# A condition-vector product moved from GpSimd columns to VectorE rows in a one-layer RWKV-7 block

## Chip, cores and metric

One core of one Trainium2 chip runs the whole kernel. The metric is device time in microseconds (us), the median of several executions; lower is better.

## The reference

One layer at width D = 2048, 512 tokens, all in float32: an RWKV-7 time mixer followed by a gated feed-forward layer with a causal convolution, each between two RMS norms. Both are modulated by a vector c:

```python
mod = jax.nn.silu(c) @ ada_w + ada_b          # ada_w: 2048 x 12288
sh_m, sc_m, g_m, sh_f, sc_f, g_f = jnp.split(mod + ada_table, 6)
h = rms(x, norm_mix_pre) * (1 + sc_m) + sh_m
y = rwkv7_mix(h)        # r, k, v = products 2048 x 2048; a scan over tokens with a 64 x 64 state per head; output product w_o
x = x + g_m * rms(y, norm_mix_post)
h = rms(x, norm_ffn_pre) * (1 + sc_f) + sh_f
x = x + g_f * rms(conv_ffn(h), norm_ffn_post)
```

The change is about `mod`: one vector times a matrix. Parts 0 and 1 (sh_m, sc_m) are needed at the start; parts 2 to 5 (g_m, sh_f, sc_f, g_f), 16 blocks of 128 channels each, are needed later and are computed beside other work.

## The kernel before, in words

Channels lie on the 128 partitions, tokens along the columns; KT = D/128 = 16. Each float32 product is made of three matmuls of halves: a weight tile is split into a high part (ScalarE, line 231) and a low part (line 233), and `mm3` (lines 276 to 278) multiplies high by high, high by low and low by high. Low parts are made by VectorE, but `wst["pool"] = 2` hands every second one to GpSimd during the state steps. Weights arrive in chunks of 512 KB through the SyncE queue (line 218).

After each `mm3` the function `tick()` advances a list of generators (`sides`) by one `yield`. Side work is placed in this way: so many ticks apart, in the order in which the code reaches it. The tile framework then orders the instructions of each engine; each engine and each DMA queue executes its own list in order, and an instruction that waits holds up those behind it. `behind()` puts an operation behind the last low part issued on VectorE.

The stages around the change: the v products (to about 300 us), the k products with the first half of the scan's preparation (`stage1`), the r products with the state steps (about 640 to 1150 us), the output product `wo`, then the feed-forward layer. In the r stage the loop over 16 blocks makes 16 r units and two gate units per block and copies the r product at line 1076. Beside it run: `inverse` (GpSimd, lines 774 and 776, small triangular inverses), `solve`, `transfer` (Gram matrices and masked copies on VectorE, lines 888 and 905) and `chain`. `chain` goes through 16 pairs of heads with eight chunks each; per chunk it multiplies the state (lines 927 and 935), scales it on ScalarE or VectorE in turn (lines 933 and 931), and yields twice. At the end of each pair `norm` begins with a square on ScalarE (line 948).

Parts 2 to 5 of `mod` come in two ways:

- `ada_jobs` (lines 460 to 508), on GpSimd. `on_pool(2048)` is 5: five groups of 512 channels, that is part 2 and a quarter of part 3. Partitions are the inputs of c. For each of 16 input blocks a 128 x 512 tile (256 KB, line 470) is loaded, multiplied by the partition's value of silu(c) (line 491; the first one at line 489) and added to a sum (line 492). The sum over partitions is four matmuls with a vector of ones (line 476) and an addition of the bias on VectorE (line 478). There are two load buffers, and four ticks between steps. It is started by `begin()` when the state steps start and must have ended at the `drain` in line 1116.
- `row_jobs` (lines 519 to 538), on VectorE. Partitions are 128 output channels and the columns are the inputs, from the transposed matrix `ada3`. One SCALAR_TENSOR_TENSOR (line 534) multiplies a row block by `crow`, the vector silu(c) on all partitions (loaded by `c_row`, line 513), and sums along the columns; line 535 adds the bias, or the earlier half. The 44 blocks that GpSimd doesn't have are made so: part 4 in the v stage (16 rows of 2048 columns), 12 rows of part 3 in the `wo` stage, part 5 at the feed-forward's output product (16 rows in two halves of 1024 columns, `in_halves`).

Of the kernel before, what the change touches and what calls it, by code (L numbers as in the profile page):

```python
# [10 lines left out]
F32 = mybir.dt.float32  # L11
F32R = mybir.dt.float32r
AF = mybir.ActivationFunctionType
ALU = mybir.AluOpType

T = 512
P = 128
# [14 lines left out]
VI = {n: i for i, n in enumerate(VEC_D)}  # L32


def on_pool(d):

    return d // min(512, d) * 2 * 5 // 8


def row_blocks(d):  # L40

    n = min(512, d) // P
    return [(vi, b) for vi in range(2, 6) for b in range(d // P) if ((vi - 2) * (d // P) + b) // n >= on_pool(d)]


class Cfg:
# [119 lines left out]
def body(ctx, tc, g, ap):  # L166
    nc = tc.nc
    KT, FT, GT, D = g.KT, g.FT, g.GT, g.D
    V, S, G, PE = nc.vector, nc.scalar, nc.gpsimd, nc.tensor
# [7 lines left out]
    def bank(i, shape=(P, T)):  # L177
        return pp.tile(list(shape), F32, tag=f"b{i}", name=f"bk{i}")
# [9 lines left out]
    ones = cp.tile([P, P], F32, name="ones")  # L188
# [9 lines left out]
    bt = cp.tile([P, 6, KT], F32, name="bt")  # L198
# [5 lines left out]
    cs = cp.tile([P, KT], F32, name="cs")  # L204
# [3 lines left out]
    mods = {q: cp.tile([P, KT], F32, name=f"mod{q}") for q in (2, 3, 4, 5)}  # L208
# [60 lines left out]
    def behind(on=True):  # L269

        return tc.issue_after(wst["last"].ins) if on else nullcontext()
# [178 lines left out]
    wst["pool"] = 0  # L450


    QC = min(512, D)
    QB = QC // P
    ROWS = row_blocks(D)

    def all_of(*vis):
        return [(vi, q) for vi in vis for q in range(D // QC)]

    def ada_jobs(pool, parts, bk, pace, bufs, eng=V, sums=1, get=None, last=False, to="ja"):  # L460

        todo = [(vi, q, k) for vi, q in parts for k in range(KT)]
        got = {}
        done = []

        def load(i):
            if i < len(todo):
                vi, q, k = todo[i]
                got[i] = get(i % bufs) if get else pool.tile([P, QC], F32, tag="js", name="js", bufs=bufs)
                nc.sync.dma_start(got[i], ap["ada2"][(vi - 2) * (D // QC) + q, :, k])  # L470

        def finish():
            vi, q, a = done.pop()
            ps = bank(bk)
            for b in range(QB):
                PE.matmul(ps[:, b:b + 1], a[:, b * P:(b + 1) * P], ones[:, 0:1], start=True, stop=True)
                yield
            V.tensor_tensor(mods[vi][:, q * QB:(q + 1) * QB], ps[:, 0:QB], bt[:, vi, q * QB:(q + 1) * QB], ALU.add)

        for i in range(bufs):  # L480
            load(i)
        yield
        for n, (vi, q, k) in enumerate(todo):
            if k == 0:
                a = pool.tile([P, QC], F32, tag=to, name="ja", bufs=sums)
            w, c = got.pop(n), cs[:, k:k + 1]
            with behind(last):
                if k == 0:
                    eng.tensor_scalar(a, w, c, None, ALU.mult)
                elif eng is G:  # L490
                    G.tensor_tensor(w, w, c.to_broadcast([P, QC]), ALU.mult)  # L491
                    G.tensor_tensor(a, a, w, ALU.add)  # L492
                else:
                    eng.scalar_tensor_tensor(a, w, c, a, ALU.mult, ALU.add)
            if eng is not G:
                load(n + bufs)
            if k >= KT // 2 and done:
                yield from finish()
            for _ in range(pace[n % len(pace)]):
                yield  # L500
            if eng is G:
                load(n + bufs)
            if k == KT - 1:
                done.append((vi, q, a))
        for _ in range(6):
            yield
        yield from finish()

    d_c = dram("d_c", (KT, P))

    part = cp.tile([P, KT], F32, name="part")
# [1 line left out]
    def c_row(t, cols=slice(0, D)):  # L513

        n = cols.stop - cols.start
        nc.sync.dma_start(t, d_c.rearrange("k p -> (k p)")[cols].unsqueeze(0).to_broadcast([P, n]))
        return t

    def row_jobs(todo, crow, get, bufs, pace, cols=slice(0, D)):

        got = {}

        def load(i):
            if i < len(todo):
                got[i] = get(i % bufs)
                nc.sync.dma_start(got[i], ap["ada3"][ROWS.index(todo[i])][:, cols])

        for i in range(bufs):
            load(i)
        yield  # L530
        for n, (vi, b) in enumerate(todo):
            w, to = got.pop(n), part[:, b:b + 1]
            with behind():
                V.scalar_tensor_tensor(w, w, 1.0, crow, ALU.mult, ALU.mult, accum_out=to)  # L534
            V.tensor_tensor(mods[vi][:, b:b + 1], to, mods[vi][:, b:b + 1] if cols.start else bt[:, vi, b:b + 1], ALU.add)
            load(n + bufs)
            for _ in range(pace):
                yield


# [42 lines left out]
    for b in range(nv0, KT - 2):  # L583
        ps = kinner("v", b, xv, bank(b % 2))
# [453 lines left out]
    s2_a, s2_b = transfer(), chain()  # L1038
    opened, jobs = [], []

    def begin():
        while fixed in sides or inv[0] in sides:
            yield
        ld_a[0], ld_b[0] = load_a(0), load_b(0)
        for i, hv in enumerate(HV):
            nc.sync.dma_start(LH[i][hv, :, HD - i * HD:P - i * HD], d_bnd[0][hv, :, 2 - 2 * i])
        while s1_last in sides:
            yield
        invert_ready(KT)
        ss_stack.close()  # L1050
        pool_of[0] = ss_stack.enter_context(tc.tile_pool(name="scn2", bufs=1))
        opened.append(True)
        wst["pool"] = 2
        ld_k[0] = load_k(0)
        yield from solve(0)
        load_v(0, 0)
        load_v(0, 1)
        jobs.append(ada_jobs(pool_of[0], [(g // (D // QC) + 2, g % (D // QC)) for g in range(on_pool(D))], 2, (4,), 2, G, 2))
        sides.extend((s2_a, s2_b, jobs[0]))

    sides.append(begin())
# [64 lines left out]
    def spare(tag, name, w=T):  # L1126
        return ap_.tile([P, w], F32, tag=tag, name=name)
# [77 lines left out]
    for b in range(KT - NL):  # L1205
        if b >= KT - NL - 4:
            fetch_x(*divmod(b - (KT - NL - 4), 2))
        ps = po[b] if b < n0 else kinner("wo", b, yx, bank((2, 6)[b % 2]))
        block_out(b, ps, acc1, yo[b], sqs[b % 2])
        if b == 1:  # L1210
            jobs = row_jobs([r for r in ROWS if r[0] < 4], c_row(spare("b2", "crow", D)),
                            lambda i: tp.tile([P, D], F32, tag=f"t3{'hl'[i]}", name="js"), 2, 8)
            sides.append(jobs)
    halves = [between(0), between(1)]
# [356 lines left out]
def layout(x):  # L1571
    D, F = x["x"].shape[-1], x["ffn_w_out"].shape[1]
    g = Cfg(D, F, x["rwkv_w1"].shape[2], x["rwkv_a1"].shape[2], x["rwkv_g1"].shape[2])
    KT, FT = g.KT, g.FT
    w = {s: x[n][0] for s, n in WMAP}
    w["r"], w["k"], w["v"] = x["rwkv_w_rkv"][0]
    tiles = np.zeros((g.nchunks * CH, P, P), np.float32)
    for i, key in enumerate(g.units):
        if key is None:
            continue  # L1580
        n, r, c = key
        t = w[n][r * P:(r + 1) * P, c * P:(c + 1) * P]
        tiles[i, :t.shape[0], :t.shape[1]] = t
    a = {"w": np.ascontiguousarray(tiles.reshape(g.nchunks, CH, P, P).transpose(0, 2, 1, 3).reshape(g.nchunks, P, CH * P))}
    ada = x["ada_w"].reshape(KT, P, 6, KT, P)
    a["ada1"] = np.ascontiguousarray(ada[:, :, 0:2].transpose(3, 1, 0, 2, 4).reshape(KT, P, KT, 2 * P))
    q = min(512, D)
    a["ada2"] = np.ascontiguousarray(
        x["ada_w"].reshape(KT, P, 6, D // q, q)[:, :, 2:].transpose(2, 3, 1, 0, 4).reshape(-1, P, KT, q)[:on_pool(D)])
    a["ada3"] = np.ascontiguousarray(np.stack([x["ada_w"][:, vi * D + b * P:vi * D + (b + 1) * P].T for vi, b in row_blocks(D)]))  # L1590
    cols = list(x["ada_b"].reshape(6, D)) + list(x["ada_table"][0].reshape(6, D))
    cols += [x[n][0] for n in ("norm_mix_pre", "norm_mix_post", "norm_ffn_pre", "norm_ffn_post")]
    cols += list(x["rwkv_mu"][0])
    cols += [x[n][0].reshape(D) for n in ("rwkv_w0", "rwkv_a0", "rwkv_k_k", "rwkv_k_a", "rwkv_r_k", "rwkv_ln_w", "rwkv_ln_b")]
    cols += [x["c"][0]]
    a["vec"] = np.ascontiguousarray(np.stack(cols).reshape(len(VEC_D), KT, P).transpose(2, 0, 1))
    f = np.concatenate([x["ffn_conv_w"][0], x["ffn_conv_b"]], 0)
    a["fvec"] = np.ascontiguousarray(f.reshape(4, 2 * FT, P).transpose(2, 0, 1))
    a["xT"] = np.ascontiguousarray(x["x"][0].T.reshape(KT, P, T))
    a["cst"] = CONST  # L1600
    return g, a
# [13 lines left out]
```

## Time and profile before

| what | value |
|---|---|
| median of 3 runs | 2754.91 us (2747.02 to 2760.35) |
| the profiled execution | 2750.25 us |
| its span in the trace | 2748.4 us |
| mean granted clock of the matrix unit | 0.979 |
| matrix unit (PE) busy | 2585.2 us (94%) |
| VectorE (DVE) busy | 2033.9 us (74%) |
| ScalarE (ACT) busy | 1329.8 us (48%) |
| GpSimd (POOL) busy | 810.1 us (29%) |

The span runs from the first to the last instruction; the profiled execution's own time is 1.85 us longer. PE is the matrix unit, PEld its weight load, DVE VectorE, ACT ScalarE, POOL GpSimd, SP SyncE; a q behind a name (SPq) is that engine's instruction queue, which issues DMAs. Matmuls are pipelined and their ends are modelled, so their busy time overstates how full the matrix unit is. In names, an arrow reads "output <- inputs": `js` is a loaded tile of the modulation matrix, `ja` a sum on GpSimd, `crow` the vector on all partitions, `wl` a low part, `wr` a loaded weight chunk, `bk` a bank of the matrix unit's results.

### The profile page before, as it was taken

How to read it: one execution, taken by the hardware profiler on the slowest of the kernel's cores; microseconds unless marked ns; L12 is line 12 of the kernel's file. 1: busy time of each engine (PE TensorE's matmuls, PEld its weight loads, DVE VectorE, ACT ScalarE, POOL GpSimd, SP SyncE). 2: the span in 40 equal slices, each digit the busy share in tenths (PEclk: the TensorE clock that was granted, in tenths of full speed). 3: DMA queues.
4: the chain of work that ended last, by engine and by line, in shares of the span. 5: the costliest groups of instructions: out<-in, count | busy, mean ns of one | idle time of the engine just before them, and what ended most of it. 6: DMA issues, size and time to landing. Idle time of an engine off the chain costs nothing.

```text
span 2748.4 us, 47108 instructions
## 1 busy us (share of the span) xinstructions
PE 2585.2 (94%) x17670; PEld 2263.7 (82%) x17670; DVE 2033.9 (74%) x3110; ACT 1329.8 (48%) x2313; POOL 810.1 (29%) x877
## 2 busy tenths in 40 slices
PE   5899999988999998999889999999999999999997
PEld 3568877776777776789779999999999988788896
DVE  5978688887666666657888888888887876544477
ACT  4442355553444445445665555555555553243464
POOL 3643114658787444500431211212111100000000
PEclk8999999999999999999999999999999999999998
DMA  8759875667767666476566776777767658532366
GB/s 298 286 195 388 288 227 194 202 207 216 192 180 190 165 170 168 138 285 227 184 207 192 193 205 187 198 197 195 205 189 198 184 178 305 194 100 93 100 203 207
DMA packets 287892, 558.69 MB, mean 203 GB/s; under 512 B 124624, under 2 KB 157776, under 8 KB 279728
## 3 DMA queue, kind: packets, MB, share of 16 engines
q1 hardware_dynamic: 257872, 444.19, 50.2%
q0 software_dynamic: 29360, 110.77, 15.1%
q8 instruction: 139, 2.28, 0.3%
q14 instruction: 89, 0.73, 0.1%
q10 hardware_dynamic: 432, 0.72, 0.1%
HBM read 477.33 MB, written 78.26 MB: 202 GB/s over the span
## 4 chain that ended last, share of the span: by engine, by line
PE 53%; DMA 9%; DVE 6%; POOL 4%; issue 3%; SPq 1%; ACT 1%; DVEq 0%; POOLq 0%; ACTq 0%
PE bk L1392 10%; PE bk L1391 10%; PE bk L1390 10%; PE bk L278 7%; PE bk L276 7%; PE bk L277 7%; DMA js<-ada 4%; DVE wl L233 1%; POOL js L491 1%; POOL ja L492 1%; DMA wr<-w 1%; PE bk L904 1%; DMA x1t<-d_x 1%; DMA tt<-d_tt 1%; DMA out<-x1t 1%
## 5 line engine op out<-in xcount | busy, mean ns | idle before, releaser
L276 PE MATMUL bk<-xh,wh 128*128 128x512 f32 (+1 forms) x2204 | 784.3, 366 | 21.0 <-ACT wh L231 5.9
L278 PE MATMUL bk<-xh,wl 128*128 128x512 f32 (+1 forms) x2204 | 767.8, 363 | 32.2 <-DVE wl L233 21.7
L277 PE MATMUL bk<-xl,wh 128*128 128x512 f32 (+1 forms) x2204 | 788.0, 362 | 2.0 <-DVE xl L1194 1.7
L231 ACT CAST wh<-wr 128x512 fp32r<-128x512 f32 x584 | 357.7, 619 | 537.9 <-PE bk L277 448.6
L233 DVE TENSOR_TENSOR wl<-wr,wh 128x512 fp32r<-128x512 f32 x518 | 381.9, 743 | 249.8 <-ACT wh L231 229.3
L278 PEld LDWEIGHTS bk<-xh,wl 128*128 128x128 f32 x2204 | 411.3, 192 | 104.7 <-DVE wl L233 32.6
L276 PEld LDWEIGHTS bk<-xh,wh 128*128 128x128 f32 x2204 | 421.2, 193 | 85.1 <-ACT wh L231 7.1
L277 PEld LDWEIGHTS bk<-xl,wh 128*128 128x128 f32 x2204 | 423.8, 193 | 63.6 <-issue 3.4
L1341 POOL DMA_DIRECT2D ss<-w x78 | 67.6, 867 | 624.7 <-DMA ss<-w 398.0
L1392 PE MATMUL bk<-xh,wl 128*128 128x256 f32 x832 | 235.7, 283 | 0.0
L1390 PE MATMUL bk<-xh,wh 128*128 128x256 f32 x832 | 235.6, 283 | 0.0
L1391 PE MATMUL bk<-xl,wh 128*128 128x256 f32 x832 | 235.6, 283 | 0.0
L1392 PEld LDWEIGHTS bk<-xh,wl 128*128 128x128 f32 x832 | 159.8, 192 | 0.1
L1390 PEld LDWEIGHTS bk<-xh,wh 128*128 128x128 f32 x832 | 159.8, 192 | 0.0
L1391 PEld LDWEIGHTS bk<-xl,wh 128*128 128x128 f32 x832 | 159.8, 192 | 0.0
L1494 POOL TENSOR_TENSOR fo<-fo,rs 128x256 f32<-128x256 f32 x4 | 3.6, 912 | 491.8 <-ACT rs L1156 491.8
L233 POOL TENSOR_TENSOR wl<-wr,wh 128x512 fp32r<-128x512 f32 x66 | 101.0, 1534 | 96.1 <-ACT wh L231 96.0
L534 DVE SCALAR_TENSOR_TENSOR js<-js,crow 128x1024 f32<-128x1024 f32 (+1 forms) x60 | 103.1, 1720 | 27.7 <-DMA js<-ada 22.2
L1390 PE MATMUL bk<-xh,wx 128*128 128x256 f32 x416 | 117.8, 283 | 0.0
L1392 PE MATMUL bk<-xh,wx 128*128 128x256 f32 x416 | 117.8, 283 | 0.0
L1391 PE MATMUL bk<-xl,wx 128*128 128x256 f32 x416 | 117.8, 283 | 0.0
L1535 DVE TENSOR_TENSOR xl<-act,xh 128x512 fp32r<-128x512 f32 (+1 forms) x172 | 92.4, 554 | 26.3 <-ACT xh L1534 26.3
(296 smaller groups left out, 5894.5 us busy)
## 6 DMA issues: line engine op xcount, KB each, us to landing
wr<-w SPq DMA_DIRECT2D x370, 512.0 KB
ss<-w SPq DMA_DIRECT2D x78, 512.0 KB
ss<-w POOLq DMA_DIRECT2D x78, 512.0 KB, 8.4
ada<-ada SPq DMA_DIRECT2D x32, 1024.0 KB
js<-ada SPq DMA_DIRECT2D x28, 1024.0 KB
js<-ada SPq DMA_DIRECT2D x80, 256.0 KB
w<-w SPq DMA_DIRECT2D x39, 512.0 KB
js<-ada SPq DMA_DIRECT2D x32, 512.0 KB
```

The lines of the kernel that those rows point to most:

```text
L231: S.copy(hi, r)
L233: ins = on.tensor_tensor(lo, r, hi.bitcast(F32), ALU.subtract)
L276: PE.matmul(out[:, cs], wh[0:kp, 0:m], xh[0:kp, cs], start=start, stop=False)
L277: PE.matmul(out[:, cs], wh[0:kp, 0:m], xl[0:kp, cs], start=False, stop=False)
L278: PE.matmul(out[:, cs], wl[0:kp, 0:m], xh[0:kp, cs], start=False, stop=stop)
L491: G.tensor_tensor(w, w, c.to_broadcast([P, QC]), ALU.mult)
L534: V.scalar_tensor_tensor(w, w, 1.0, crow, ALU.mult, ALU.mult, accum_out=to)
L1341: G.dma_start(t[:, i], chunk(j, other), accum_op=ALU.add)
L1390: PE.matmul(ps, wh, xh, start=start and k == 0, stop=False, skip_group_check=True)
L1391: PE.matmul(ps, wh, xl, start=False, stop=False, skip_group_check=True)
L1392: PE.matmul(ps, wl, xh, start=False, stop=k == CH - 1, skip_group_check=True)
L1535: V.tensor_tensor(ahl[e][1][:, cs], act[f][:, cs], ahl[e][0][:, cs].bitcast(F32), ALU.subtract)
```

## The change

`on_pool`, `ada_jobs` and the array `ada2` are gone, and `row_blocks` lists all 64 blocks. In their place, at the same point of `begin()`, a new generator `scan_rows` makes the first 20 row blocks (part 2 and a quarter of part 3) by `row_jobs`, in two halves of 1024 columns, with one load buffer, eight ticks a row and the next load issued two ticks (`lag`) after a product. The `wo` stage's 12 rows and the other jobs are the same blocks as before.

```diff
 def row_blocks(d):
-    n = min(512, d) // P
-    return [(vi, b) for vi in range(2, 6) for b in range(d // P) if ((vi - 2) * (d // P) + b) // n >= on_pool(d)]
+    return [(vi, b) for vi in range(2, 6) for b in range(d // P)]
...
-    def ada_jobs(pool, parts, bk, pace, bufs, eng=V, sums=1, get=None, last=False, to="ja"):
...
-    def row_jobs(todo, crow, get, bufs, pace, cols=slice(0, D)):
+    def row_jobs(todo, crow, get, bufs, pace, cols=slice(0, D), lag=0):
...
             V.tensor_tensor(mods[vi][:, b:b + 1], to, mods[vi][:, b:b + 1] if cols.start else bt[:, vi, b:b + 1], ALU.add)
+            for _ in range(lag):
+                yield
             load(n + bufs)
-            for _ in range(pace):
+            for _ in range(pace - lag):
                 yield
...
+    def scan_rows():
+        for cols in (slice(0, D // 2), slice(D // 2, D)):
+            row = c_row(c2("crow", 1, (P, D // 2)), cols)
+            yield from row_jobs(ROWS[:KT + KT // 4], row, lambda i: c2("js", 1, (P, D // 2)), 1, 8, cols, 2)
...
-        jobs.append(ada_jobs(pool_of[0], [(g // (D // QC) + 2, g % (D // QC)) for g in range(on_pool(D))], 2, (4,), 2, G, 2))
+        jobs.append(scan_rows())
         sides.extend((s2_a, s2_b, jobs[0]))
...
-            jobs = row_jobs([r for r in ROWS if r[0] < 4], c_row(spare("b2", "crow", D)),
+            jobs = row_jobs(ROWS[KT + KT // 4:2 * KT], c_row(spare("b2", "crow", D)),
                             lambda i: tp.tile([P, D], F32, tag=f"t3{'hl'[i]}", name="js"), 2, 8)
```

## Rows read from the trace of the kernel before

**Rows 1.** Busy time by stage: stretch, us, busy of PE, PEld, DVE, ACT, POOL, clock, DMA share, GB/s.
```profile
680.00:1150.00 470.00, 437.59 (x3670) 349.72 (x3669) 315.95 (x501) 208.54 (x404) 290.47 (x269) 0.95 0.66 177
1150.00:1250.00 100.00, 100.00 (x487) 81.21 (x486) 59.51 (x91) 40.94 (x73) 2.05 (x2) 1.00 0.69 251
```
**Rows 2.** Groups of GpSimd, 680 to 1150 us: busy, mean ns | idle before, releaser.
```profile
L492 POOL TENSOR_TENSOR ja<-ja,js 128x512 f32<-128x512 f32 x74 | 102.6, 1386 | 2.8
L491 POOL TENSOR_TENSOR js<-js,cs 128x512 f32<-128x512 f32 x75 | 87.3, 1168 | 79.8 <-DMA js<-ada 79.6
L233 POOL TENSOR_TENSOR wl<-wr,wh 128x512 fp32r<-128x512 f32 x31 | 42.2, 1361 | 54.6 <-ACT wh L231 54.6
```
**Rows 3.** Waits, 680 to 1150 us, SyncE's own among them: us, times, longest.
```profile
POOL js L491 <- DMA js<-ada: 79.6, 35, 7.7
...
PE bk L278 <- POOL wl L233: 9.9, 5, 3.9
...
SPq L470 <- POOL ja L492: 41.5, 26, 4.4
...
SPq L218 <- DVE wl L233: 20.5, 10, 5.4
```
**Rows 4.** The chain that ended last, 680 to 1150 us, by line.
```profile
by line: issue 8.4%; POOL js L491 6.0%; PE bk L276 5.9%; PE bk L278 5.7%; POOL ja L492 5.7%; DMA js<-ada 5.3%; PE bk L277 5.2%; PE bk L904 4.6%; DMA tt<-d_tt 3.8%; PE bk L852 3.3%; PE bk L935 3.0%; POOL wl L233 3.0%; POOL it L774 2.5%; PE b
```
**Rows 5.** Two stretches, line 276 alone: us, PE, PEld, clock, DMA share, GB/s.
```profile
720.00:900.00 180.00, 48.27 (x115) 22.47 (x114) 0.96 0.68 185
940.00:990.00 50.00, 14.04 (x34) 6.40 (x34) 1.00 0.53 137
```
**Rows 6.** The same two stretches, line 935 alone.
```profile
720.00:900.00 180.00, 19.59 (x172) 13.08 (x172) 0.96 0.68 185
940.00:990.00 50.00, 5.77 (x52) 3.81 (x52) 1.00 0.53 137
```
**Rows 7.** ScalarE in order of time: squares after a head pair, last r copy.
```profile
716.20 0.60 ACT L948 ACTIVATE sqy<-bk 128x512 f32<-128x512 f32 x1 [3.51 <-PE bk L935]
...
917.14 0.59 ACT L948 ACTIVATE sqy<-bk 128x512 f32<-128x512 f32 x1
...
950.88 0.60 ACT L948 ACTIVATE sqy<-bk 128x512 f32<-128x512 f32 x1
...
1005.74 0.59 ACT L948 ACTIVATE sqy<-bk 128x512 f32<-128x512 f32 x1
...
1058.92 0.58 ACT L1076 COPY rsb<-bk 128x512 f32<-128x512 f32 x1
```
**Rows 8.** VectorE's low parts, 720 to 917 us, then 940 to 990 us.
```profile
L233 DVE TENSOR_TENSOR wl<-wr,wh 128x512 fp32r<-128x512 f32 x15 | 19.1, 1275 | 10.7 <-ACT wh L231 10.7
...
L233 DVE TENSOR_TENSOR wl<-wr,wh 128x512 fp32r<-128x512 f32 x4 | 2.8, 690 | 2.6 <-ACT wh L231 2.6
```
**Rows 9.** Line 476: matmuls, ns shortest/median/longest, first and last start.
```profile
L476 PE MATMUL bk<-ones,ja x40: 166/250/271, 863.8 to 1198.4; 128*128 128x1 f32 x40
```
**Rows 10.** Groups of VectorE, 2290 to 2380 us: busy, mean ns | idle before.
```profile
L534 DVE SCALAR_TENSOR_TENSOR js<-js,crow 128x1024 f32<-128x1024 f32 x28 | 34.2, 1224 | 22.0 <-DMA js<-ada 17.6 <-DMA crow<-d_c 4.4
...
L535 DVE TENSOR_TENSOR mod<-part,mod 128x1 f32<-128x1 f32 x16 | 2.5, 155 | 0.1
L534 DVE DVE_READ_ACCUMULATOR js<-js,crow 128x1 f32 x28 | 2.3, 83 | 0.0
```
**Rows 11.** Tile js, 2290 to 2380 us: its engine's idle time by releaser, times.
```profile
  DMA js<-ada: 17.6, 20
  DMA crow<-d_c: 4.4, 1
```
**Rows 12.** Chain, 2290 to 2380 us, the longest load of js: start, us.
```profile
2307.64 5.70 DMA js<-ada
```
**Rows 13.** Tile js, 190 to 630 us: shortest/median/longest ns, first and last.
```profile
L534 DVE SCALAR_TENSOR_TENSOR js<-js,crow x16: 2274/2285/2296, 223.5 to 325.8; 128x2048 f32<-128x2048 f32 x16
```
**Rows 14.** Tile js, 680 to 1150 us: GpSimd's idle time by releaser, times.
```profile
  DMA js<-ada: 82.8, 37
```

More of the change, by code (lines that the diff above doesn't have):

```diff
@@ L32 @@
 VI = {n: i for i, n in enumerate(VEC_D)}
-def on_pool(d):
-    return d // min(512, d) * 2 * 5 // 8
 def row_blocks(d):
-    n = min(512, d) // P
-    return [(vi, b) for vi in range(2, 6) for b in range(d // P) if ((vi - 2) * (d // P) + b) // n >= on_pool(d)]
+    return [(vi, b) for vi in range(2, 6) for b in range(d // P)]
 class Cfg:
@@ L450, in body @@
     wst["pool"] = 0
-    QC = min(512, D)
-    QB = QC // P
     ROWS = row_blocks(D)
-    def all_of(*vis):
-        return [(vi, q) for vi in vis for q in range(D // QC)]
-    def ada_jobs(pool, parts, bk, pace, bufs, eng=V, sums=1, get=None, last=False, to="ja"):
[L462 to L507, printed above, removed]
     d_c = dram("d_c", (KT, P))
@@ L1586, in layout @@
     a["ada1"] = np.ascontiguousarray(ada[:, :, 0:2].transpose(3, 1, 0, 2, 4).reshape(KT, P, KT, 2 * P))
-    q = min(512, D)
-    a["ada2"] = np.ascontiguousarray(
-        x["ada_w"].reshape(KT, P, 6, D // q, q)[:, :, 2:].transpose(2, 3, 1, 0, 4).reshape(-1, P, KT, q)[:on_pool(D)])
     a["ada3"] = np.ascontiguousarray(np.stack([x["ada_w"][:, vi * D + b * P:vi * D + (b + 1) * P].T for vi, b in row_blocks(D)]))
```

## The prediction

> **What bounds the kernel now.** The page's busy shares come first, but a busy matrix unit is not one at its peak, so I cut the span by stages and look for the one that the change touches. GpSimd is busy 290 of 470 us between 680 and 1150 us, the state steps, and 2 of the 100 us after them [rows 1]. In the first stretch the granted clock is 0.95, in the second 1.00: the matrix unit pauses in the state steps and is full right after. So the argument is about these 470 us; before and after them GpSimd has no operation of the kind that goes.
>
> What fills GpSimd there [rows 2]: 74 additions and 75 multiplies for the condition vector, and between them 31 low parts of weights, for which the matrix unit waits. The waits show the snag [rows 3]: GpSimd stood idle 79.6 us for the loads of its multiplies, and its queue is in order, so a low part that is issued behind such a multiply is late. The matrix unit itself names that line for only 9.9 us. The chain of waits names more: multiplies 6.0%, additions 5.7%, their loads 5.3% of the stretch [rows 4], 17.0% of 470 us or 80 us.
>
> **Part 1: the GpSimd products go.** The bounds are 10 us (the direct waits [rows 3]) and 80 us (the chain [rows 4]); the upper is too high, because behind each of these pieces stands another wait. Between them the trace holds an experiment of its own: from 940 to 990 us GpSimd had almost nothing of this. First measure, the work done per microsecond: the first of the three matmuls of a weight block ran 115 times in 180 us (0.639 per us) beside a loaded GpSimd and 34 times in 50 us (0.680) beside a quiet one, 6.4% more [rows 5]; the matmuls of the state's output went from 172 in 180 us (0.956) to 52 in 50 us (1.040), 8.8% more [rows 6]. The mean, 7.6% faster, saves 7.1% of the time. Second measure, spacing: the steps of one head pair end 33.5 us apart in the loaded stretch (716.20 to 917.14, six pairs) and 27.4 us apart in the other (950.88 to 1005.74, two pairs) [rows 7], 18% less; with the 6% that the weight blocks save by their count, and the matrix unit dividing its time between the two, 12%. The last r product is copied at 1058.92 [rows 7]; from 680 to some 1070 us, less the quiet 50, 340 us are affected. 7.1% of that is 24 us, 12% is 41 us; nothing speaks for one measure more than for the other, so I take **33 us saved**. Two things are in it and are not added again: VectorE's own slowdown beside GpSimd (its low parts took 1275 ns each in the loaded stretch and 690 in the quiet one [rows 8]), and the 41.5 us that SyncE stood waiting for GpSimd's additions before it could issue the next load [rows 3].
>
> **Part 2: the matmuls that summed GpSimd's groups go.** 40 records at a median of 250 ns [rows 9] are 10 us if each stood alone, and nothing if they lay beside other waits. They are pipelined and the last of them run at 1198 us where the matrix unit is full; I take **2 us saved**.
>
> **Part 3: 40 products on VectorE come,** 20 rows in two halves of 1024 columns. The same form runs at the end of the kernel: 1224 ns, 83 ns to read its sum, 155 ns for the addition behind it [rows 10]. 40 x 1462 ns = 58 us. If all of it fell into idle time it would cost 0, if none 58. VectorE is idle 154 of the 470 us [rows 1]; on the other side it carries half of the state from chunk to chunk, and its queue is in order. The cover is its idle time, and part 1 enlarges it: 15 low parts at 585 ns less are 9 us in 197 us [rows 8]. I take a fifth, nearer to the low end, **12 us lost**; without that cover it would be the 58.
>
> **Part 4: VectorE may wait for these loads.** Behind a waiting product stand, in VectorE's queue, low parts of weights, the masked copies and the state steps, and for them waits the matrix unit. The bytes don't change (80 x 256 KB, now 40 x 512 KB). There is one buffer; the next load is issued two ticks after a product (a tick is a step of three matmuls) and the product stands six ticks behind it. The old job had 80 x 4 ticks, 5 x 4 for its sums and seven more, 347 ticks in 470 us, 1.35 us each; so the lead is 8 us. At the end of the kernel loads of the same 512 KB stand in the chain with up to 5.70 us [rows 12]. That leaves over 2 us of slack, which SyncE spends when it stands at a weight load first: 20.5 us in 10 waits in this stretch [rows 3]. The bounds come from two places with the same operation: 0 (16 products from 190 to 630 us, no wait listed [rows 13]) and the end of the kernel, 17.6 us [rows 11] for 28 products [rows 10], so 25 us for 40, and 4.4 us for each of two loads of the vector [rows 11], 34 us in all. The lead here is nearer to the first place; I take 11 us of waiting, half of it on the path: **6 us lost**.
>
> **Queues that the work is moved past.** SyncE issues 42 transfers in place of 80; its waits are in part 1 already, so I price this at nothing, and without that cover it would still be a gain. GpSimd's stores keep their order and find a shorter queue. The job takes 2 x (1 + 20 x 8) = 322 ticks against 347, so the drain at the end of the stage gets nothing new to wait for. The two later jobs (12 rows of 2048 columns, 16 rows in halves) stay as they are.
>
> **Sum.** -33 - 2 + 12 + 6 = -17 us. The profiled execution took 2750.25 us, so 2733 for it; it lies 4.66 us under the median of the runs, 2754.91, and for the median I forecast **2738 us**.
>
> **A rule against it.** 290.5 - 102.6 - 87.3 = 101 us of GpSimd's work stay [rows 1, 2], a fifth of the stretch. If each of the 40 products met one of these operations with that chance and one of the two lost 1224 ns, 10 us would go, and the sum would be -7: 2748. The Trainium skill, page SBUF — State Buffer, section "SBUF: two separate sides", says that VectorE and GpSimd hold one shared port pair as an exclusive lock, also when a VectorE operation has two SBUF inputs, and that the loser waits for the whole instruction; by it the new products block GpSimd's low parts. The 1275 and 690 ns of rows 8 agree that the two hinder each other; which one loses, they don't show.
>
> **The rivals.**
> 1. *VectorE waits where GpSimd did* (slower, 0.22). Place: part 4. With one buffer a late load makes the product late, that makes SyncE's next load late, and weight loads stand behind it on SyncE. For it: GpSimd waited 82.8 us for its 80 loads of half the size [rows 14]. Two such waits per new row are 83 us; half on the path, 41 us in place of my 6, gives -33 - 2 + 12 + 41 = +18: 2773. Against it: the lead of 8 us and the stage from 190 to 630 us. It decides from 37 us on the path, 1.9 us of waiting a row; from there the time is over 0.5% above.
> 2. *GpSimd doesn't pace the stage* (same, 0.25). Only the direct 10 us come back: -10 - 2 + 12 + 6 = +6, or 0 if no load is late; 2757. For it: the quiet stretch also had less DMA traffic, 137 against 185 GB/s [rows 5], so the gain of part 1 may be the traffic's.
> 3. *The shared port* (same, 0.08), as worked out: 2748.
> 4. *Everything hides* (in the forecast's 0.45): 41 + 2 us saved, nothing lost, 2712.
>
> **How the numbers follow.** A measurement of this kernel can't tell less than 0.5%, 13.8 us, from no change. The forecast at -17 is faster, with 0.45; same is 0.25 + 0.08 = 0.33; slower 0.22. The range goes from rival 4, 2712, to rival 1 at its price, 2773, and leaves out that one's worse half and a little below. The forecast's own range is 2712 to 2741.
>
> **What would show it.** Right: in the stretch GpSimd's busy time falls by some 190 us, VectorE's low parts go towards 690 ns, head pairs end some 30 us apart, products wait under 0.5 us each for their loads, and the stretch ends 15 to 20 us sooner with all behind it as long as before. Wrong: VectorE waits 60 us or more for the loads, the new products and their loads make a tenth of the stretch's chain, or head pairs stay 33 us apart beside an idle GpSimd.

## The result and the profile after

The changed kernel takes 2732.13 us (median of 4; 2727.24 to 2733.26), the kernel before 2755.80 us in the same session: a ratio of 0.9914, 95% interval 0.9887 to 0.9942, that is 24 us less. The forecast was 2738. The profiled execution took 2731.33 us, its span is 2729.5 us, 18.9 us shorter than before.

Busy time in the state steps after the change, the columns of rows 1:

```profile
680.00:1150.00 470.00, 443.39 (x3767) 354.49 (x3768) 335.47 (x637) 218.64 (x424) 97.17 (x116) 0.97 0.68 182
```

Against [rows 1], GpSimd's busy time falls from 290 to 97 us, VectorE's rises by only 20, and the matrix unit starts 97 matmuls more in the same 470 us.

ScalarE's square at the end of a head pair (line 889 is the 948 of before) and the last copy of an r product, in order of time, after the change:

```profile
714.06 0.60 ACT L889 ACTIVATE sqy<-bk 128x512 f32<-128x512 f32 x1 [0.38 <-PE bk L876]
...
913.99 0.60 ACT L889 ACTIVATE sqy<-bk 128x512 f32<-128x512 f32 x1
...
1041.31 0.60 ACT L1022 COPY rsb<-bk 128x512 f32<-128x512 f32 x1
...
1156.92 0.60 ACT L889 ACTIVATE sqy<-bk 128x512 f32<-128x512 f32 x1 [2.17 <-PE bk L876]
```

The last pair of the kernel before, the same view:

```profile
1176.89 0.60 ACT L948 ACTIVATE sqy<-bk 128x512 f32<-128x512 f32 x1 [0.81 <-PE bk L935]
```

The state steps end 20.0 us sooner, and the span is 18.9 us shorter: the whole gain is made there, and what follows gives 1 us back. The r products end 17.6 us sooner (1058.92 in [rows 7]). In the stretch that I had called loaded, six pairs still take 200 us (714.06 to 913.99; before, 201), and the gain shows in the r products beside them and in the pairs behind. From the first to the last pair it is 442.9 us, 29.5 a pair, against 460.7 us.

Groups of VectorE in the state steps after the change, 680 to 1150 us, and its low parts from 720 to 917 us (busy, mean ns | idle before, releaser):

```profile
L473 DVE SCALAR_TENSOR_TENSOR js<-js,crow 128x1024 f32<-128x1024 f32 x40 | 50.8, 1270 | 24.7 <-DMA js<-ada 24.6
```
```profile
L227 DVE TENSOR_TENSOR wl<-wr,wh 128x512 fp32r<-128x512 f32 x16 | 11.5, 720 | 4.6 <-ACT wh L225 4.4
```

The 40 products stand at a mean of 1270 ns (1224 in [rows 10]) and waited 24.6 us for loads. VectorE's low parts are at a mean of 720 ns where they were at 1275 [rows 8].

Waits of the matrix unit and of SyncE from 680 to 1150 us after the change (us, times, longest), and the chain of that stretch by line:

```profile
PE bk L272 <- POOL wl L227: 3.4, 1, 3.4
...
SPq L212 <- DVE wl L227: 64.5, 23, 10.6
...
SPq L465 <- DVE js L473: 14.5, 11, 4.3
```
```profile
by line: PE bk L270 13.4%; PE bk L272 12.2%; PE bk L271 12.0%; PE bk L845 10.1%; DMA tt<-d_tt 6.7%; PE bk L876 6.2%; PE bk L793 6.1%; PE bk L826 4.4%; DMA js<-ada 2.8%; PE bk L868 2.8%; PE bk L776 2.3%; issue 2.0%; PE bk L785 1.8%; PE bk L7
```

The 17% that the GpSimd products and their loads had in [rows 4] are gone. The new loads have 2.8%; the three matmul lines of the weights go from 16.8% to 37.6%. SyncE waits for the products 14.5 us where it waited 41.5 us for GpSimd's additions [rows 3]; its waits for VectorE's low parts rise from 20.5 to 64.5 us.

### The profile page after: what moved, and what is told of

It is laid out like the page before. It is cut to its first block, busy times and chain, and to the rows that moved or that the text cites. A ratio compares the mean times of both kernels' runs of the same rounds, so it can differ in the third digit from the quotient of the medians.

```text
span 2729.5 us, 46869 instructions
## 1 busy us (share of the span) xinstructions
PE 2573.4 (94%) x17630; PEld 2253.4 (83%) x17630; DVE 2041.8 (75%) x3225; ACT 1329.7 (49%) x2313; POOL 610.8 (22%) x722
## 4 chain that ended last, share of the span: by engine, by line
PE 57%; DMA 10%; DVE 5%; issue 2%; ACT 1%; POOL 1%; SPq 1%; DVEq 0%; ACTq 0%; POOLq 0%
PE bk L1338 10%; PE bk L1336 10%; PE bk L1337 10%; PE bk L270 7%; PE bk L272 7%; PE bk L271 7%; DMA js<-ada 4%; PE bk L845 2%; DMA act<-d_act 1%; DMA tt<-d_tt 1%; PE bk L876 1%; PE bk L793 1%; DVE wl L227 1%; DVE js L473 1%; DMA wr<-w 1%
## 5 line engine op out<-in xcount | busy, mean ns | idle before, releaser
L227 DVE TENSOR_TENSOR wl<-wr,wh 128x512 fp32r<-128x512 f32 x518 | 368.9, 717 | 238.3 <-ACT wh L225 221.5
L473 DVE SCALAR_TENSOR_TENSOR js<-js,crow 128x1024 f32<-128x1024 f32 (+1 forms) x100 | 153.8, 1540 | 59.0 <-DMA js<-ada 53.5
```

The lines of the kernel that those rows point to most:

```text
L227: ins = on.tensor_tensor(lo, r, hi.bitcast(F32), ALU.subtract)
```

## The experiments

Twelve kernels, each timed in five rounds beside the kernel before. Ratios are to that kernel in the same session, with a 95% interval. To compare sessions I use ratios: 0.1% is 2.75 us.

**1. No job at all** (from the kernel before):

```diff
-        jobs.append(ada_jobs(pool_of[0], ...))
+        jobs.append(iter(()))
+        V.tensor_copy(mods[2], bt[:, 2])
+        V.tensor_copy(mods[3][:, 0:4], bt[:, 3, 0:4])
```

> The kernel before without any condition-vector job in the state steps (part 2 and a quarter of part 3 of the modulation get the bias alone). Both theories, the queue (low parts of weights stood behind GpSimd multiplies that waited for loads) and the port (GpSimd's operations slow VectorE's), expect all of the gain here: the kernel before less 33 to 42 us, 2714 to 2723, as the changed kernel (2732) still pays 12 to 18 us for its products on VectorE. If the products on VectorE are free, it is 2732 like the changed kernel; if the stage isn't paced by GpSimd, 2745 or more.

Measured: 2710.30 us, ratio 0.9844 (0.9826 to 0.9863), 43 us less than before. This is the floor: GpSimd's products, their loads and sums cost 43 us, and the 40 products on VectorE with theirs cost the difference to the changed kernel, 0.70% or 19 us (22 by medians). In its trace six pairs of the loaded stretch take 170 us, and the state steps end at 1135.08:

```profile
714.98 0.60 ACT L948 ACTIVATE sqy<-bk 128x512 f32<-128x512 f32 x1 [1.67 <-PE bk L935]
...
885.08 0.60 ACT L948 ACTIVATE sqy<-bk 128x512 f32<-128x512 f32 x1
...
1135.08 0.60 ACT L948 ACTIVATE sqy<-bk 128x512 f32<-128x512 f32 x1 [0.81 <-PE bk L935]
```

So GpSimd's products had cost some 31 us there (201 against 170), and in the changed kernel, where the same six pairs take 200, the new products and their loads take that room again.

**2. All low parts on VectorE, GpSimd's products kept** (from the kernel before):

```diff
-        wst["pool"] = 2
+        wst["pool"] = 0
```

> The kernel before with all low parts of weights on VectorE in the state steps; GpSimd keeps its products and loads. Queue theory: no matmul can stand behind GpSimd's products any more, so most of the gain comes back, less 31 low parts on VectorE: 2730 to 2740. Port theory: VectorE is hindered as before and has 31 operations more: 2755 to 2770.

Measured: 2732.12 us, ratio 0.9931 (0.9908 to 0.9955). So without touching the products, 19 us come back by taking the low parts off GpSimd, although VectorE gets 31 operations more. It is the queue theory's number.

**3. GpSimd's products without loads** (from the kernel before):

```diff
+                if i >= bufs:
+                    got[i] = first[i % bufs]
+                    return
-                got[i] = get(i % bufs) if get else pool.tile(...)
+                got[i] = first[i] = get(i % bufs) if get else pool.tile(...)
                 nc.sync.dma_start(got[i], ap["ada2"][...])
```

> The kernel before with GpSimd's products, but only the first two tiles loaded and used again (the sums are not those of the modulation matrix). Queue theory: the 80 us of waits for loads in GpSimd's queue go, its 200 us of products stay: 2730 to 2740. Port theory: the same operations hinder VectorE as long: 2750 to 2756. If the traffic of the loads is what cost (20 MB less), it is 2735 or less, and e4 falls by as much.

Measured: 2758.90 us, ratio 1.0016 (1.0003 to 1.0030): no gain, against the queue theory as I had stated it. GpSimd's waits for its multiplies' loads are gone, but VectorE's own low parts are slower than in the kernel before (mean 1432 ns against 1100). The medians below say that this comes from a few long ones. VectorE's low parts from 680 to 1130 us (number, then shortest, median and longest in ns), first in the kernel before, then in this run:

```profile
L233 DVE TENSOR_TENSOR wl<-wr,wh x32: 619/776/2412, 690.4 to 1127.1; 128x512 fp32r<-128x512 f32 x32
```
```profile
L233 DVE TENSOR_TENSOR wl<-wr,wh x31: 620/693/7733, 692.5 to 1081.8; 128x512 fp32r<-128x512 f32 x31
```

So the edit changed two things at once. With each low part paired in order with its high part, the time from the end of the high part to the end of the low part falls on GpSimd from a mean of 2.68 to 1.88 us (680 to 1150 us) and rises on VectorE from 2.48 to 3.28 us: what the one engine's low parts gained, the other's lost. The run shows that taking the 80 us of waits away gives nothing back; it does not show that they cost nothing.

**4. VectorE's products without loads** (from the changed kernel; one tile is loaded per half):

```diff
+                if lag and i:
+                    got[i] = got[0]
+                    return
...
-            w, to = got.pop(n), part[:, b:b + 1]
+            w, to = got[n] if lag else got.pop(n), part[:, b:b + 1]
...
-                V.scalar_tensor_tensor(w, w, 1.0, crow, ...)
+                V.scalar_tensor_tensor(w, w, 0.0 if lag else 1.0, crow, ...)
```

> The changed kernel with its 40 products on VectorE, but one tile loaded per half and used again, multiplied by zero (so part 2 and a quarter of part 3 get the bias alone). What is lost to VectorE's 24.6 us of waits for loads comes back: with half of it on the path 12 us, 2720; if VectorE's idle time covers the waits, 2730 to 2733.

Measured: 2727.47 us, ratio 0.9913 (0.9894 to 0.9931), the changed kernel's 0.9914. VectorE's 24.6 us of waits for loads, and the loads' traffic, cost nothing that can be measured.

**5. Neither job nor low parts on GpSimd** (both edits, of the first and the second run):

> No condition-vector job in the state steps (as the first run) and all low parts on VectorE (as the second). Against the first run (2710) it prices 31 low parts moved to VectorE with nothing on GpSimd but the inverse: at 0.7 us each they are 22 us of VectorE time, at the share of 0.38 that the 40 products showed, 8 us: 2718. Against the second run (2732) it prices GpSimd's products with no low part behind them: with the port, some 14 us; without it, the second run would stand at 2718 as well, which it doesn't, so 2732 here would mean that the low parts alone, not the port, make up the second run's rest.

Measured: 2718.28 us, ratio 0.9870 (0.9847 to 0.9893). 31 low parts moved to VectorE cost 0.26% or 7 us (8 expected), which is not clear of the noise. The second run is 0.61% or 17 us above this one; the two differ by GpSimd's products, with their loads and sums, and no low part stands behind them. VectorE's low parts take a mean of 877 ns there and 709 here.

**6. GpSimd's products without loads, low parts on VectorE** (the edits of the second and third runs):

> GpSimd's products on tiles loaded once (as the third run; the sums are not those of the modulation matrix), and all low parts on VectorE. No low part stands behind GpSimd and no load is waited for, so what it is above the run with neither is the port alone. Queue theory: as that run, some 2718, and 40 us under the third run (2759). Port theory: the third run's slow VectorE stays and gets 31 operations more, 2755 or above.

Measured: 2775.49 us, ratio 1.0073 (1.0048 to 1.0098), 2.03% or 56 us above the run before this one. No low part is behind GpSimd, only the first two tiles are loaded, and yet it is the slowest of all: the products alone, by what they do to VectorE. Its low parts (two SBUF inputs; number, shortest, median and longest) and its masked copies out of the matrix unit's banks (one SBUF input; number, busy, mean), 680 to 1130 us, first in the run with neither, then in this one, and there also its products of r with the decay (two SBUF inputs):

```profile
L233 DVE TENSOR_TENSOR wl<-wr,wh x72: 673/692/1148, 695.5 to 1129.8; 128x512 fp32r<-128x512 f32 x72
...
L888 DVE TENSOR_TENSOR rh<-bk,cst 64x512 f32<-64x512 f32 x60 | 41.2, 686 | 2.5 <-PE bk L885 1.2
```
```profile
L233 DVE TENSOR_TENSOR wl<-wr,wh x61: 673/692/23380, 694.4 to 1115.4; 128x512 fp32r<-128x512 f32 x61
...
L877 DVE TENSOR_TENSOR ri<-rsb,E x28: 673/689/18935, 698.7 to 1108.2; 64x512 f32<-64x512 f32 x28
...
L891 DVE TENSOR_TENSOR rh<-bk,cst 64x512 f32<-64x512 f32 x52 | 35.7, 687 | 1.2 <-PE bk L888 0.2
```

The masked copies are the same to a nanosecond. The means of the other two nearly double (709 to 1284 and 723 to 1505 ns), but not their medians: the low parts' is 692 ns in both runs. A few operations make the means, one low part of 23.38 us and one product of r of 18.94 us above all. Here is that low part, and what all engines did meanwhile (the columns of rows 1):

```profile
738.93 23.38 DVE L233 TENSOR_TENSOR wl<-wr,wh 128x512 fp32r<-128x512 f32 x1 [1.04 <-ACT wh L231]
```
```profile
738.93:762.31 23.38, 5.59 (x35) 4.32 (x33) 23.38 (x1) 1.82 (x4) 22.82 (x26) 0.72 0.10 17
```

VectorE did nothing else, GpSimd ran 26 operations one right behind the other, and the matrix unit was busy for 5.59 us and waited 17.8 us for this low part, which ended when GpSimd's string did. That is the hindrance between the two engines shown by itself: not a slower VectorE, but single operations with two SBUF inputs that stand still. The two longest are 42 us together, of the 56; the profiled execution is the slowest of this run's eight (2789.41 us).

**7. Low parts on VectorE in the changed kernel:** `wst["pool"] = 2` becomes 0.

> The changed kernel with all low parts on VectorE. Queue theory: GpSimd's queue is free in the changed kernel, so its low parts gain something there; moved to VectorE beside the 40 products they cost 8 to 15 us: 2740 to 2747. If port and GpSimd's slow low parts (1340 ns against 700) cost as much as they relieve: 2732.

Measured: 2730.57 us, ratio 0.9917 (0.9896 to 0.9939), the changed kernel's own. With its queue free, GpSimd's low parts gain nothing that can be measured there any more.

**8. Low parts all on GpSimd in the changed kernel:** `wst["pool"] = 2` becomes 1.

> The changed kernel with all low parts of the state steps on GpSimd, which is idle three quarters of that time. If VectorE's load is what is left of the cost (22 us above the run without a job), 24 us less on VectorE give back a third or more: 2722 to 2726. If the latency of a low part counts, 1340 against 700 ns each, matmuls wait for it: 2735 to 2745.

Measured: 2745.74 us, ratio 0.9969 (0.9951 to 0.9986), 0.55% or 15 us worse than the changed kernel. GpSimd's low parts and the matrix unit's wait for them, 680 to 1150 us:

```profile
L227 POOL TENSOR_TENSOR wl<-wr,wh 128x512 fp32r<-128x512 f32 x62 | 88.1, 1421 | 225.9 <-ACT wh L225 221.5 <-PE bk L826 3.6 <-DMA wr<-w 0.9
```
```profile
PE bk L272 <- POOL wl L227: 7.1, 4, 4.9
```

GpSimd is idle most of the time and yet the wrong place: a low part takes 1421 ns there and 701 to 720 on VectorE. The matmul waits 7.1 us for GpSimd where it waited 3.4; how the other part of the 15 us comes about isn't shown.

**9. Each product made twice** (from the changed kernel):

```diff
                 V.scalar_tensor_tensor(w, w, 1.0, crow, ALU.mult, ALU.mult, accum_out=to)
+                if lag:
+                    V.scalar_tensor_tensor(w, w, 1.0, crow, ALU.mult, ALU.mult, accum_out=spare_sum)
```

> The changed kernel with each of its 40 products in the state steps made twice (the second one's sum is not used), no further loads. If the 22 us that the products cost against the run without a job are VectorE's time at a share on the path (58 us at 0.38), another 40 x 1.3 us = 52 us cost 20 us or, as the idle time is used up, more: 2752 to 2760. If they are the loads, the traffic and SyncE's queue, it stays at 2732 to 2736.

Measured: 2751.29 us, ratio 0.9985 (0.9971 to 0.9999), 0.71% or 20 us above the changed kernel. The added operations:

```profile
L476 DVE SCALAR_TENSOR_TENSOR js<-js,crow 128x1024 f32<-128x1024 f32 x37 | 48.0, 1298 | 0.3
```

40 x (1298 + 80) ns are 55 us of VectorE time; 20 of them reach the end, a share of 0.36. The first set, 58 us, cost 19 us, 0.33. Each of the two shares is uncertain by some 9 us; both sets together, against the first run, cost 1.41% or 39 us of 113, 0.34, uncertain by some 7 us. So the products' price is VectorE's time, at about a third, and no rise shows with the second set.

**10. Four rows moved to the v stage** (from the changed kernel; the state steps keep 16 rows, the v stage makes 20 at seven ticks):

```diff
-    jobs = row_jobs([r for r in ROWS if r[0] == 4], crow, ..., 2, 9)
+    jobs = row_jobs([r for r in ROWS if r[0] == 4] + ROWS[KT:KT + KT // 4], crow, ..., 2, 7)
...
-            yield from row_jobs(ROWS[:KT + KT // 4], row, ...
+            yield from row_jobs(ROWS[:KT], row, ...
```

> The changed kernel with four of the 20 rows (the quarter of part 3) moved from the state steps to the v stage, which takes 20 rows at seven ticks in place of 16 at nine. In the v stage the matrix unit is full beside such products, so a fifth of the 22 us should come back there: 2728. If the v stage, whose DMA engines are busy 0.9 to 1.0, stalls instead, 2732 to 2745.

Measured: 2735.26 us, ratio 0.9923 (0.9905 to 0.9941): no gain. In the state steps the first and last pairs end at

```profile
721.38 0.60 ACT L889 ACTIVATE sqy<-bk 128x512 f32<-128x512 f32 x1
...
1154.70 0.60 ACT L889 ACTIVATE sqy<-bk 128x512 f32<-128x512 f32 x1 [0.81 <-PE bk L876]
```

so the pairs take 433.3 us in place of 442.9, but the first ends 7.3 us later: what the state steps win has been spent before them.

**11. No lag** (from the changed kernel; the last argument of `row_jobs` in `scan_rows` is 0 in place of 2):

> The changed kernel with the next load issued right after each product (lag 0) in place of two ticks later. The lag keeps SyncE from standing at the load until the product has read the buffer, with weight loads behind. If that matters, SyncE waits longer and the time rises by 3 to 10 us, 2735 to 2742; as the run without loads gained little, I expect under 4 us either way, 2728 to 2736.

Measured: 2730.50 us, ratio 0.9907 (0.9888 to 0.9926), no difference. SyncE's wait for the products, 680 to 1150 us, is 19.3 us, 5 us longer, and costs nothing that can be measured.

**12. Four rows moved to the output product's stage** (from the changed kernel):

```diff
-            yield from row_jobs(ROWS[:KT + KT // 4], row, ...
+            yield from row_jobs(ROWS[:KT], row, ...
...
-            jobs = row_jobs(ROWS[KT + KT // 4:2 * KT], c_row(spare("b2", "crow", D)), ..., 2, 8)
+            jobs = row_jobs(ROWS[KT:2 * KT], c_row(spare("b2", "crow", D)), ..., 2, 6)
```

> The changed kernel with four of the 20 rows moved from the state steps to the output product's stage, which takes 16 rows at six ticks in place of 12 at eight. The matrix unit is full there, so a fifth of the 22 us that the products cost in the state steps should come back: 2728. If that stage's loads (DMA engines busy 0.8, 1 MB a row) come late and the end of its job is waited for, 2732 to 2740.

Measured: 2725.86 us, ratio 0.9907 (0.9885 to 0.9929). The median is the lowest of the kernels that compute everything, 6 us under the changed kernel's, but the intervals lie over each other; that it beats the changed kernel isn't shown.

## Why the prediction came out, step by step

**The place was right.** The gain lies in the state steps, which end 20.0 us sooner, and the rest keeps its length to 1 us.

**Part 1, 33 us, and part 2, 2 us: both mechanisms are there, and the size was too small.** The first run measures both parts together: 43 us, where the sum had 35. The runs split them in two. The products with no low part behind them: second run against fifth, 17 us, with slower low parts on VectorE (877 against 709 ns). The other 26 us come only where half of the low parts are made on GpSimd beside the products: the kernel before is 19 us above the second run, which in turn pays 7 us for its low parts on VectorE. Part 1 held both, the queue as its reason and VectorE's slowdown as included.

The weak step is "GpSimd stood idle 79.6 us for the loads, and its queue is in order". In the kernel before, the 31 low parts on GpSimd began 41.0 us in all after their high parts were ready (without the job, 25.7 us for 32). In 24.3 of these 41.0 us GpSimd was busy with the products, and in only 4.2 us did it stand idle for a load. So a low part seldom stood behind an idle wait, and mostly behind the work. The third run doesn't settle what the waits cost: without them the low parts on GpSimd began 16.2 us late in all, but VectorE lost as much. And with all low parts on VectorE the run without waits was 1.42% or 39 us slower (sixth run against second): GpSimd no longer paused, and VectorE stood still. That the 26 us are lateness in the queue fits these numbers, but is not shown: low parts on GpSimd also keep that engine busy beside VectorE.

The quiet stretch from 940 to 990 us was a fair guide: 24 us by counts and 41 us by spacing, against 43 measured. Taking the middle was a choice without a reason. The first run bears the second measure out: without the job six pairs of the loaded stretch come 28.4 us apart, 15% closer than before, where the measure had 18%.

**Part 3, 12 us, was too small.** The products cost 19 us of their 58 us (0.33), and a second set 20 us of 55 (0.36), where I had taken a fifth. The reason that I gave for the low share, idle time enlarged by the relief, holds for VectorE's total, which rose by 20 us only, but about a third of each product's time reached the end all the same.

**Part 4, 6 us, was wrong in both factors.** VectorE waited 24.6 us, not 11, and nothing that can be measured reached the end (0.9913 without loads, 0.9914 with them). My lead of 8 us left more late loads than I thought, ten of 40. That no cost shows is measured; why the waits are free isn't. SyncE's queue, priced at nothing, was worth nothing that can be measured: without the lag it waits longer for the products, and the kernel takes the same time.

**The sum** forecast 17 us, and 24 were measured: the gain was 43 for 35, the costs 19 for 18. That the costs came out is luck: part 3 was 7 us too small and part 4 6 us too large.

**The rivals.** The first one's place was right, its price was not: waits of 24.6 us and no loss that can be measured. The second falls with the first run: 43 us hung on the job, and the loads' traffic, which the changed kernel keeps, isn't what cost (fourth run). The third, the shared port, came out with its sign turned: GpSimd's low parts didn't suffer (1361 ns before [rows 2], 1338 after), the new products' mean rose by 46 ns, 2 us in all and not 10 (their median is 1218 ns, so it was a few of them). The hindrance was a cost of the kernel before: it goes with the 17 us. The Trainium skill (page SBUF — State Buffer, section "SBUF: two separate sides") says that a VectorE operation with two SBUF inputs and a GpSimd operation that reads SBUF exclude each other, and that the loser is blocked for the whole instruction of the other. The sixth run agrees on whom it hits: operations with two SBUF inputs stood up to 23.38 us, those with one input from the matrix unit's banks took a mean of 687 ns as against 686. It goes beyond it in how long: the loser stood through 26 instructions, not one.

**What would show it:** GpSimd fell by 193 us (190 expected), the low parts went to 720 ns, the products waited 0.6 us each (under 0.5 expected), and the pairs came 29.5 us apart on average. But up to 914 us they stayed 33.3 us apart beside a GpSimd with little to do, which I had named as a sign of being wrong. It was a bad sign: it left out that the new products would take the room that GpSimd gave back there (170 us without them, 200 with them).

**What stays open.** The tile framework orders each engine's list anew for every kernel, so each difference between two runs contains a new order as well; the split of 26 and 17 us is made of differences of ratios whose intervals are 5 to 6.5 us either way, so each of the two is uncertain by some 10 us.

## What to carry to other kernels

An engine that looks idle is no free helper: price what stands behind its operations in its own queue, and what they do to the engine beside it. A wait in such a queue isn't a cost until something is shown to be late by it, so look for what stood behind it; taking the wait away in an experiment can change a second thing as well, as it did here. Read a mean together with its median and longest: a doubled mean was a few operations that stood still. And operations moved to an engine that is two thirds busy cost about a third of their duration here, not a fifth.

## What the runs showed of the hardware that was not expected

A VectorE operation with two SBUF inputs stood still through a whole string of GpSimd operations, 23.38 us through 26 of them in the sixth run. How long GpSimd is busy didn't decide it, but whether it pauses. From 680 to 1130 us GpSimd was busy 252.93 us in the second run and 209.53 us in the sixth. But the products of the second run waited for their loads, and there the longest low part on VectorE took 2.82 us:

```profile
L233 DVE TENSOR_TENSOR wl<-wr,wh x65: 674/691/2819, 693.8 to 1115.6; 128x512 fp32r<-128x512 f32 x65
```

In the kernel before, no VectorE operation from 680 to 1150 us took over 3.2 us. In the third run, which took the waits away from it, a copy took 11.6 us and low parts 7.7 and 7.4 us. In each of these long ones GpSimd's operations followed one another with at most 27 ns between them until just before the end. So the waits for loads, which I had read as the snag, were also what let VectorE in. How long a pause has to be isn't shown.
